# Half-height TensorE products made 128 rows high in a two-layer hybrid block

## The chip, the cores and the metric

The kernel runs on one core of a Trainium2 chip. The metric is the device time of one execution in microseconds (us); the time stated for a kernel is the median of its runs.

## The reference

Two layers over 512 latent tokens and 256 context tokens of width 1024. Each layer normalises its input, projects it with one matrix `w_in`, and feeds three token mixers: an RWKV-7 recurrence in both directions (4 heads of 64), a windowed attention with grouped queries (8 query heads on 2 key heads of 64, blocks of 128 tokens, a sink logit), and a 2-D Fourier mix. Their outputs are projected, weighted by sigmoid gates, summed and projected again; then comes a gated FFN with a convolution of width 3. The parts that the change touches:

```
for d, (xw, xa) in enumerate(((xw_f, xa_f), (xw_b, xa_b))):        # per direction
    w_log = -softplus(-(w0[d] + tanh(xw) @ w2[d])) - 0.5           # xw, xa: 64 columns each
    a = sigmoid(a0[d] + xa @ a2[d])
...
S = S * w_t + (S @ -kk_t) b_t^T + v_t k_t^T ;  y_t = S r_t         # recurrence, per head of 64
...
s_w = einsum("bqhgd,bkhd->bhgqk", q_b, k_b) * ATT_SCALE            # scores, d = 64
g = sigmoid(xg) @ g2                                               # gate of the recurrence's output
```

All is computed in float32; the large products run in a faster float32 form (named F32R in the code), each operand split in a high and a low part.

## The kernel before

All work is cut into 128-partition tiles; for each layer the order is: `w_in`'s first columns, the recurrence, the attention, the merge and output projection, the FFN. The code is straight-line Python without loops on the chip. Tiles come from pools with a fixed number of buffers, and a list scheduler sets the order of the instructions on each engine when the kernel is built, from the order of the program, the priorities (`tc.high_priority()` around the recurrence) and estimated durations. Once built, each engine works through its own list in order and waits on semaphores. DMAs are issued from SyncE (SP) in order, too.

**Background work.** The gates and branches of `mix` (`work`, a generator) and the modulation vectors (`bg`, `mods_few`) are interleaved with the recurrence and the attention. `wload` brings 128-column weights: a DMA to `wr`, ScalarE writes `wh`, GpSimd (POOL) or VectorE (DVE) writes `wl`; `gemm3` (L177 to L179) multiplies three times.

**The recurrence.** Tokens go in windows of 128, each direction d has one, six windows per layer (two of context, four of latents). `wkv_features` makes a window's operands: two LoRA products per direction (L808, over the 64 rows of direction d of `w2`, `a2`), activations, then for each head half h (rows 64h to 64h+63 hold one head of each pair) `W1[h]` (L846 on DVE, L848 on POOL) and `BK` (L849, L850 on DVE), four products `BK x W1[h]` over those 64 rows (L859), and DVE writes the masked results to `MR` (L864) and into the other 64 rows of `W1[h]` (L865), which `wkv_step` then uses at full height (L1016, L1042). `W1` has four buffers, so a window takes those of two windows before. `wkv_scan` inverts a small triangular matrix (`wkv_inverse`) and does two steps of 64 tokens (`wkv_prep`, `wkv_step`). Window w+1's features stand in the program ahead of window w's scan. `rwkv_readout` normalises the output and multiplies by a gate that comes from `g2` (L1098).

A float32 product stands in the trace as two weight loads and two matmuls; an F32R product as one of each.

**The scores.** `stacked` loads 64 rows of a query head twice, in partitions 0 to 63 and 64 to 127; the query tile holds the high part above and the low part below. The keys' `hi` is the high part in both halves, and `lo` the low part in the upper 64 rows alone. `scores` multiplies, for each of two heads and each group of key blocks, `qh` by `kh` over 128 rows (L1215) and by `kl` over the first 64 rows (L1216), adds masks (L1218) and the sink column (L1221). Softmax follows on DVE, ScalarE (ACT) and POOL, then `values` transposes (L1251) and multiplies (L1261) for the item before.

`cond` makes `sT` (SiLU of the conditioning vectors, 32 columns per k, of which two are not zero); TensorE reads it in `mods`, DVE as a scalar in `mods_bg` and `mods_few` (L293).

Of the kernel before, what the change touches and what calls it, by code (L numbers as in the profile page):

```python
# [7 lines left out]
F32 = mybir.dt.float32  # L8
# [3 lines left out]
ALU = mybir.AluOpType  # L12
# [8 lines left out]
KD = D // 128  # L21
# [42 lines left out]
class Kern:  # L64
# [117 lines left out]
    def setup(self):  # L182
# [18 lines left out]
        nc.gpsimd.memset(self.mT[1], 0.0)  # L201
        self.sT = self.t(cp, [128, KD, 32], "sT")
        self.mrow = [tc.dram_tile([3, 2, D], F32, name=f"mrow{l}") for l in range(DEPTH)]
# [4 lines left out]

    def cond(self):

        p = self.pool("condp", side="right")
        c = self.t(p, [128, 2, KD], "c")
        self.nc.sync.dma_start(out=c, in_=self.I["cond"])
        self.nc.vector.memset(self.sT, 0.0)
        self.act(self.sT[:, :, 0:2].rearrange("p k s -> p s k"), c, AF.Silu)
        p.release()

# [31 lines left out]
    def mods_bg(self, which, pool, tag="x", bufs=3):  # L249
# [3 lines left out]
        for l, r, ns in which:  # L253
            acc = [[self.t(pool, [128, 1024], "ma", bufs=4) for _ in range(2)] for _ in range(ns)]
            for k in range(KD):
                for g in range(2):
                    mw = self.t(pool, [128, 1024], "mw", bufs=bufs)
                    c0 = r * 2048 + g * 1024
                    nc.sync.dma_start(out=mw, in_=self.I["mod_w"][l, k * 128:(k + 1) * 128, c0:c0 + 1024])
                    for s in range(ns):  # L260
                        a, v = acc[s][g], self.sT[:, k, s:s + 1]
                        if k == 0:
                            nc.vector.tensor_scalar(a, mw, v, None, ALU.mult)
                        else:
                            nc.vector.scalar_tensor_tensor(a, mw, v, a, ALU.mult, ALU.add)
                    yield
# [9 lines left out]
    def mods_few(self, which, pool, tag):  # L276
# [3 lines left out]
        for l, r, c, ns in [(l, r, c, ns) for l, r, ns in which for c in range(8)]:  # L280
            c0 = r * 2048 + c * 256
            acc = [self.t(pool, [128, 256], "ma", bufs=4) for _ in range(ns)]
            for k in range(KD):
# [4 lines left out]
                for s in range(ns):  # L288
                    v = self.sT[:, k, s:s + 1]
                    if k == 0:  # L290
                        nc.vector.tensor_scalar(acc[s], mw[:, 0], v, None, ALU.mult)
                    else:
                        nc.vector.scalar_tensor_tensor(acc[s], mw[:, k % 4], v, acc[s], ALU.mult, ALU.add)  # L293
# [389 lines left out]
    def rwkv_params(self, l, pool):  # L683
        nc, I = self.nc, self.I
        w2 = self.t(pool, [128, RWKV_DIM], "w2")
        nc.sync.dma_start(out=w2, in_=I["rwkv_w2"][l].rearrange("d k c -> (d k) c"))
        a2 = self.t(pool, [128, RWKV_DIM], "a2")
        nc.sync.dma_start(out=a2, in_=I["rwkv_a2"][l].rearrange("d k c -> (d k) c"))
        g2 = self.t(pool, [128, RWKV_DIM], "g2")
        nc.sync.dma_start(out=g2, in_=I["rwkv_g2"][l])  # L690
        V = self.V1[l]
# [11 lines left out]
        if l > 0:  # L703
            nc.vector.tensor_scalar(x[:, 23:25], V[:, V_V0:V_V0 + 2], 0.5, None, ALU.mult)
        return dict(w2=w2, a2=a2, g2=g2, x=x)

# [70 lines left out]
    def wkv_features(self, l, w, F, P, wp, wt):  # L777
# [17 lines left out]
        for d in range(2):  # L795
# [5 lines left out]
            def tok(t):  # L801
                return flip(t[:, :, lo:lo + WT])

            pp = self.ps()
            for z, (lw, xx) in enumerate(((P["w2"], F["xw"]), (P["a2"], F["xa"]))):
                for k in range(2):
                    c = (2 * z + k) * WT
                    nc.tensor.matmul(pp[:, c:c + WT], lhsT=lw[64 * d:64 * d + 64, k * 128:(k + 1) * 128],  # L808
                                     rhs=xx[64 * d:64 * d + 64, lo:lo + WT], start=True, stop=True)
            sw = self.t(wt, [128, 2, WT], "wt")  # L810
# [22 lines left out]
            if need_y:  # L833
# [3 lines left out]
                else:  # L837
                    nc.gpsimd.tensor_tensor(kb, kb, kf, ALU.add)
            W1 = [self.t(wp, [128, NC, 2, 128], f"W1{h}", bufs=4) for h in range(2)]
            BK = self.t(wp, [128, NC, 2, 128], "BK", bufs=4)  # L840
# [15 lines left out]
            for h in range(2):  # L856
                ps = self.ps()
                for q in range(4):
                    nc.tensor.matmul(ps[:, q * 128:q * 128 + m], lhsT=rows(BK, h)[:, q // 2, q % 2, :],  # L859
                                     rhs=rows(W1[h], h)[:, q // 2, q % 2, 0:m], start=True, stop=True)  # L860
                pv = ps.rearrange("p (q t) -> p q t", q=4)[:, :, 0:m]
# [198 lines left out]
    def rwkv_readout(self, l, F, P, out, tmp):  # L1060
# [5 lines left out]
        parts = (("l", 0, TL), ("c", TL, TC))[:len(halves)]  # L1066
        n = TT if l == 0 else TL
        dv = self.t(tmp, [128, 2, TT], "dv", bufs=1)
        va = self.t(tmp, [128, 2, TT], "va", bufs=1)
# [15 lines left out]
        for k in range(2):  # L1085
# [10 lines left out]
            for o, w in halves:  # L1096
                ps = self.ps()
                nc.tensor.matmul(ps[:, :w], lhsT=P["g2"][:, k * 128:(k + 1) * 128], rhs=F["xg"][:, o:o + w], start=True,  # L1098
                                 stop=True)
# [56 lines left out]
    def stacked(self, src, o, n, pool, tag, bufs, keys=False):  # L1156
# [10 lines left out]
        lo = self.t(pool, [128, TT], tag + "l", F32R, bufs=bufs)  # L1167
        nc.vector.tensor_tensor(lo[0:64, :n], d[0:64, :n], hi[0:64, :n].bitcast(F32), ALU.subtract)
        return hi, lo
# [25 lines left out]
    def scores(self, l, t, i, qa, ka, pool):  # L1195
# [8 lines left out]
        for hh in range(2):  # L1204
# [4 lines left out]
            for first, n, c in ((blks[0], nw, c0), (4, 2, 512)):  # L1209
# [5 lines left out]
                nc.tensor.matmul(o, lhsT=qh[:, qs], rhs=kh[:, ks], start=True, stop=False)  # L1215
                nc.tensor.matmul(o, lhsT=qh[0:64, qs], rhs=kl[0:64, ks], start=False, stop=not masked)  # L1216
                for z in masked:
# [340 lines left out]
    def run(self):  # L1558
# [5 lines left out]
        p0 = self.pool("modp", side=B)  # L1564
        self.cond()
        tiles = []
# [234 lines left out]
```

## Time and profile before

| | |
|---|---|
| runs | 2569.32, 2578.45, 2600.42 us; median 2578.45 |
| the profiled execution | 2573.11 us, of which the span is 2571.3 us |
| mean granted TensorE clock | 0.948 of full |
| busy in the span | PE 93%, PEld 76%, DVE 73%, ACT 41%, POOL 37% |
| DMA | 251.35 MB, mean 98 GB/s |

PE is TensorE's matmuls and PEld its weight loads, which can run beside matmuls. A matmul's end is modelled and consecutive matmuls overlap in the profile, so the time that one takes out of a stream is read from the start of one to the start of the next (called its slot here), not from its duration. Times in the views are us from the span's start.

### The profile page before, as it was taken

The numbers are of one execution on the slowest core, as the hardware profiler recorded it, in microseconds if no ns is written. First come the engines' busy times: TensorE is split into PE (matmuls) and PEld (weight loads), VectorE is DVE, ScalarE is ACT, GpSimd is POOL, SyncE is SP. The second block draws the span as 40 slices with busy tenths as digits, with TensorE's granted clock in tenths as the row PEclk, the third lists the DMA queues.
The fourth block names the chain that finished last, engine by engine and source line by source line (L and its number), as shares of the span: only waits on it lengthen the run. The fifth ranks groups of instructions, "written<-read, shape, count | busy, mean of one in ns | idle before, by whom it ended". The sixth has DMA issues, their size and how long they took to land. (4 is left out here: it accounts for less than half of the span.)

```text
span 2571.3 us, 43544 instructions
## 1 busy us (share of the span) xinstructions
PE 2379.3 (93%) x16612; PEld 1957.7 (76%) x16612; DVE 1882.8 (73%) x3458; ACT 1054.6 (41%) x2156; POOL 941.1 (37%) x908
## 2 busy tenths in 40 slices
PE   7898999999999979999999888999989998899997
PEld 4766777787777768899898776667767776888886
DVE  5966776827765577878878845788666866999988
ACT  3243343334433445334333534435334434544443
POOL 4442322023333264333333543333123434545553
PEclk9988989999989989999999998789989999999999
DMA  7611111743324222122122421111264544333321
GB/s 236 191 50 44 48 41 36 221 129 116 117 80 144 95 70 79 58 69 72 60 74 64 135 86 58 54 46 59 63 207 142 155 129 138 105 96 99 99 87 58
DMA packets 284464, 251.35 MB, mean 98 GB/s; under 512 B 14460, under 2 KB 241236, under 8 KB 284256
## 3 DMA queue, kind: packets, MB, share of 16 engines
q1 hardware_dynamic: 284256, 248.57, 30.8%
q8 instruction: 131, 2.15, 0.3%
q14 instruction: 77, 0.63, 0.1%
HBM read 221.23 MB, written 27.29 MB: 97 GB/s over the span
## 5 line engine op out<-in xcount | busy, mean ns | idle before, releaser
L177 PE MATMUL mm<-at,wh 128*128 128x256 f32 (+2 forms) x1968 | 675.5, 344 | 15.8 <-DVE v L612 7.1
L179 PE MATMUL mm<-at,wl 128*128 128x256 f32 (+2 forms) x1968 | 670.7, 341 | 7.7 <-DVE wl L118 5.5
L178 PE MATMUL mm<-at,wh 128*128 128x256 f32 (+2 forms) x1968 | 668.9, 340 | 9.6 <-POOL at L118 6.9
L118 POOL TENSOR_TENSOR wl<-wr,wh 128x512 fp32r<-128x512 f32 (+1 forms) x248 | 343.1, 1390 | 490.8 <-ACT wh L106 459.2
L177 PEld LDWEIGHTS mm<-at,wh 128*128 128x128 f32 x1968 | 388.2, 197 | 53.4 <-issue 7.9
L178 PEld LDWEIGHTS mm<-at,wh 128*128 128x128 f32 x1968 | 387.5, 197 | 43.7 <-POOL at L118 10.8
L179 PEld LDWEIGHTS mm<-at,wl 128*128 128x128 f32 x1968 | 387.2, 197 | 36.8 <-DVE wl L118 7.3
L106 ACT ACTIVATE wh<-wr 128x512 fp32r<-128x512 f32 (+1 forms) x342 | 204.3, 605 | 229.3 <-PE mm L178 127.0
L118 DVE TENSOR_TENSOR wl<-ws,wh 128x512 fp32r<-128x512 f32 x176 | 166.8, 949 | 62.8 <-ACT wh L106 62.8
L177 PE MATMUL x<-dh,hid 128*128 128x512 f32 x440 | 177.7, 404 | 27.9 <-DVE acc L602 26.5
L293 DVE SCALAR_TENSOR_TENSOR ma<-mw,sT,ma 128x256 f32<-128x256 f32 x336 | 184.9, 590 | 11.7 <-DMA mw<-in_mod_w 9.1
L179 PE MATMUL x<-dh,hid 128*128 128x512 f32 x440 | 172.8, 394 | 1.1 <-DVE hid L118 1.1
L178 PE MATMUL x<-dl,hid 128*128 128x512 f32 x440 | 172.9, 393 | 0.0
L602 DVE TENSOR_TENSOR acc<-x,acc 128x512 f32<-128x512 f32 x200 | 134.4, 683 | 23.4 <-PE x L179 22.9
L118 POOL TENSOR_TENSOR dl<-dr,dh 128x1024 fp32r<-128x1024 f32 x44 | 112.0, 2545 | 81.6 <-ACT dh L106 76.6
L106 ACT ACTIVATE wh<-ws 128x512 fp32r<-128x512 f32 x170 | 103.7, 623 | 85.6 <-PE mm L178 67.5
L177 PEld LDWEIGHTS x<-dh,hid 128*128 128x128 f32 x440 | 83.1, 189 | 54.5 <-DVE acc L602 37.4
L106 ACT ACTIVATE P<-P,st 128x513 f32<-128x513 f32 (+5 forms) x120 | 86.1, 722 | 81.8 <-DVE P L1227 70.9
L178 PE MATMUL x<-at,wh 128*128 128x512 f32 (+2 forms) x312 | 114.9, 368 | 5.0 <-POOL at L118 3.0
L177 PE MATMUL x<-at,wh 128*128 128x512 f32 (+2 forms) x312 | 116.2, 373 | 1.5 <-DVE mT L311 0.8
L154 POOL TENSOR_TENSOR ws<-wr,wr 128x512 f32<-128x512 f32 x42 | 66.2, 1577 | 139.6 <-DVE wl L118 138.9
L179 PE MATMUL x<-at,wl 128*128 128x512 f32 (+2 forms) x312 | 114.8, 368 | 0.0
(486 smaller groups left out, 4811.9 us busy)
## 6 DMA issues: line engine op xcount, KB each, us to landing
mw<-in_mod_w SPq DMA_DIRECT2D x96, 512.0 KB
wr<-in_ffn_up SPq DMA_DIRECT2D x176, 256.0 KB
wr<-in_w_in SPq DMA_DIRECT2D x164, 256.0 KB
dr<-in_ffn_down SPq DMA_DIRECT2D x44, 512.0 KB
gd<-sg SPq DMA_DIRECT2D x32, 256.0 KB
wraw<-in_w_out SPq DMA_DIRECT2D x32, 256.0 KB
hd<-h SPq DMA_DIRECT2D x32, 256.0 KB
h<-hd SPq DMA_DIRECT2D x28, 256.0 KB
```

Of the source, the lines that this page charges most:

```text
L106: return self.nc.scalar.activation(out, in_, func, **kw)
L118: e.tensor_tensor(lo, full, hi.bitcast(F32), ALU.subtract)
L154: e.tensor_tensor(raw[m], raw[x], raw[y], op)
L177: mm(ps, lhsT=lh, rhs=rh, start=first and k == 0, stop=False)
L178: mm(ps, lhsT=lh, rhs=rl, start=False, stop=False)
L179: mm(ps, lhsT=ll, rhs=rh, start=False, stop=last and k == nk - 1)
L293: nc.vector.scalar_tensor_tensor(acc[s], mw[:, k % 4], v, acc[s], ALU.mult, ALU.add)
L602: nc.vector.tensor_tensor(acc[i][:, cs], ps, acc[i][:, cs], ALU.add)
```

## The change

`scores` multiplies `qh` by `kl` over all 128 rows, and `stacked` fills the lower 64 rows of `lo` as well. `w2` and `a2` get one copy per direction, each with 64 rows of zeros, so that L808 runs over 128 rows; the products of `BK` and `W1[h]` (L859) run over 128 rows, with `W1[h]`'s other 64 rows set to zero by POOL at the start of a direction's features. The load of `g2` moves from `rwkv_params` into `rwkv_readout`. `sT` moves into a pool that is released early, and `s2` keeps its two columns that DVE reads.

```diff
-        self.sT = self.t(cp, [128, KD, 32], "sT")
+        self.s2 = self.t(cp, [128, KD, 2], "s2")
...
-    def cond(self):
+    def cond(self, pool):
+        self.sT = self.t(pool, [128, KD, 32], "sT", bufs=1)
...
         self.act(self.sT[:, :, 0:2].rearrange("p k s -> p s k"), c, AF.Silu)
+        self.nc.gpsimd.tensor_copy(self.s2, self.sT[:, :, 0:2])
...
-        w2 = self.t(pool, [128, RWKV_DIM], "w2")
-        nc.sync.dma_start(out=w2, in_=I["rwkv_w2"][l].rearrange("d k c -> (d k) c"))
-        a2 = self.t(pool, [128, RWKV_DIM], "a2")
-        nc.sync.dma_start(out=a2, in_=I["rwkv_a2"][l].rearrange("d k c -> (d k) c"))
-        g2 = self.t(pool, [128, RWKV_DIM], "g2")
-        nc.sync.dma_start(out=g2, in_=I["rwkv_g2"][l])
+        w2, a2 = (self.t(pool, [128, 2, RWKV_DIM], m) for m in ("w2", "a2"))
+        for m, src in ((w2, I["rwkv_w2"]), (a2, I["rwkv_a2"])):
+            for d in range(2):
+                nc.gpsimd.memset(m[64 - 64 * d:128 - 64 * d, d], 0.0)
+                nc.sync.dma_start(out=m[64 * d:64 * d + 64, d], in_=src[l, d])
...
+            W1 = [self.t(wp, [128, NC, 2, 128], f"W1{h}", bufs=4) for h in range(2)]
+            for h in range(2):
+                nc.gpsimd.memset(rows(W1[h], 1 - h)[:, :, :, 0:m], 0.0)
...
-                    nc.tensor.matmul(pp[:, c:c + WT], lhsT=lw[64 * d:64 * d + 64, k * 128:(k + 1) * 128],
-                                     rhs=xx[64 * d:64 * d + 64, lo:lo + WT], start=True, stop=True)
+                    nc.tensor.matmul(pp[:, c:c + WT], lhsT=lw[:, d, k * 128:(k + 1) * 128], rhs=xx[:, lo:lo + WT],
+                                     start=True, stop=True)
...
-                    nc.tensor.matmul(ps[:, q * 128:q * 128 + m], lhsT=rows(BK, h)[:, q // 2, q % 2, :],
-                                     rhs=rows(W1[h], h)[:, q // 2, q % 2, 0:m], start=True, stop=True)
+                    nc.tensor.matmul(ps[:, q * 128:q * 128 + m], lhsT=BK[:, q // 2, q % 2, :],
+                                     rhs=W1[h][:, q // 2, q % 2, 0:m], start=True, stop=True)
...
+        g2 = self.t(tmp, [128, RWKV_DIM], "g2", bufs=1)
+        nc.sync.dma_start(out=g2, in_=self.I["rwkv_g2"][l])
...
-        nc.vector.tensor_tensor(lo[0:64, :n], d[0:64, :n], hi[0:64, :n].bitcast(F32), ALU.subtract)
+        nc.vector.tensor_tensor(lo[:, :n], d[:, :n], hi[:, :n].bitcast(F32), ALU.subtract)
...
-                nc.tensor.matmul(o, lhsT=qh[0:64, qs], rhs=kl[0:64, ks], start=False, stop=not masked)
+                nc.tensor.matmul(o, lhsT=qh[:, qs], rhs=kl[:, ks], start=False, stop=not masked)
```

## Rows read from the trace of the kernel before

**Rows 1.** The page's first part: busy time, share of the span, instructions.
```profile
PE 2379.3 (93%) x16612; PEld 1957.7 (76%) x16612; DVE 1882.8 (73%) x3458; ACT 1054.6 (41%) x2156; POOL 941.1 (37%) x908
```

**Rows 2.** Windows: length, busy (instructions) PE, PEld, DVE, ACT, POOL; clock; DMA.
```profile
565.00:805.00 240.00, 234.67 (x1485) 178.85 (x1484) 155.77 (x391) 102.42 (x233) 77.37 (x67) 0.97 0.35 107
1880.00:2085.00 205.00, 199.80 (x1140) 148.94 (x1140) 140.25 (x308) 88.73 (x185) 74.79 (x66) 0.97 0.51 156
140.00:480.00 340.00, 311.97 (x3504) 245.10 (x3503) 245.66 (x579) 137.85 (x324) 98.84 (x161) 0.89 0.19 59
1560.00:1880.00 320.00, 294.51 (x3130) 218.03 (x3130) 234.73 (x557) 139.06 (x321) 87.67 (x147) 0.87 0.21 66
```

**Rows 3.** Timeline of PE, one head's scores: start, us, then the instruction (rows*columns, operand).
```profile
638.62 0.28 PE L179 MATMUL x<-yh,wl 128*128 128x256 f32 x1
638.73 0.34 PE L1215 MATMUL s<-ka,qa 128*128 128x384 f32 x1
639.00 0.44 PE L1216 MATMUL s<-kal,qa 64*128 64x384 f32 x1
639.38 0.23 PE L1218 MATMUL s<-mprev,identb 128*128 128x128 bf16 x1
...
639.47 0.36 PE L1215 MATMUL s<-ka,qa 128*128 128x256 f32 x1
639.76 0.38 PE L1216 MATMUL s<-kal,qa 64*128 64x256 f32 x1
640.08 0.18 PE L1221 MATMUL s<-sink,onesb 128*128 128x1 bf16 x1
```

**Rows 4.** Timeline of PEld, the weight load of one second product.
```profile
639.00 0.18 PEld L1216 LDWEIGHTS s<-kal,qa 64*128 64x128 f32 x1 [0.19 <-issue]
```

**Rows 5.** Timeline of PE in the FFN, full-height products with 384 columns.
```profile
1004.73 0.34 PE L177 MATMUL mm<-at,wh 128*128 128x384 f32 x1
1004.90 0.34 PE L178 MATMUL mm<-at,wh 128*128 128x384 f32 x1
```

**Rows 6.** Groups by line and form: count, busy us, mean ns, idle before and its releasers.
```profile
L1216 PE MATMUL s<-kal,qa 64*128 64x256 f32 x112 | 44.0, 393 | 0.3 <-DVE kal L1168 0.3
L1216 PE MATMUL s<-kal,qa 64*128 64x384 f32 x32 | 15.1, 471 | 0.0
```

**Rows 7.** Timeline of PE in the recurrence: one group of eight, one of sixteen half-height matmuls.
```profile
303.70 0.71 PE L808 MATMUL x<-xw,w 64*128 64x128 f32 x4
304.25 0.61 PE L808 MATMUL x<-xa,a 64*128 64x128 f32 x4
304.79 0.50 PE L177 MATMUL mm<-at,wh 128*128 128x512 f32 x1
...
318.36 0.28 PE L178 MATMUL mm<-at,wh 128*128 128x256 f32 x1
318.57 1.71 PE L859 MATMUL x<-W,BK 64*128 64x128 f32 x16
320.21 0.39 PE L179 MATMUL mm<-at,wl 128*128 128x256 f32 x1
320.44 0.28 PE L177 MATMUL mm<-at,wh 128*128 128x256 f32 x1
```

**Rows 8.** Groups by line and form, L859 on PE: idle before it and releasers.
```profile
L859 PE MATMUL x<-W,BK 64*128 64x128 f32 x320 | 46.5, 302 | 22.8 <-DVE BK L850 13.5 <-POOL W L848 8.7 <-DVE BK L849 0.6
L859 PE MATMUL x<-W,BK 64*128 64x64 f32 x64 | 11.3, 332 | 9.3 <-DVE BK L849 5.8 <-DVE BK L850 3.4
```

**Rows 9.** Timeline of POOL: a memset, and the two products of one direction's features.
```profile
293.06 0.31 POOL L905 MEMSET T<- 128x256 f32 x1 [2.79 <-ACT iv L106]
...
299.44 1.71 POOL L848 TENSOR_TENSOR W<-r,e 64x256 f32<-64x256 f32 x2
```

**Rows 10.** Timelines of SP and PE at the start of layer 2's readout.
```profile
1860.35 1.40 SPq L1478 DMA_DIRECT2D back<-zd  x3
...
1868.94 0.70 PE L1098 MATMUL x<-xg,g 128*128 128x512 f32 x1 [0.35 <-DVE bo L1093]
```

More of the change, by code (lines that the diff above doesn't have):

```diff
@@ L260, in mods_bg @@
                     for s in range(ns):
-                        a, v = acc[s][g], self.sT[:, k, s:s + 1]
+                        a, v = acc[s][g], self.s2[:, k, s:s + 1]
                         if k == 0:
@@ L288, in mods_few @@
                 for s in range(ns):
-                    v = self.sT[:, k, s:s + 1]
+                    v = self.s2[:, k, s:s + 1]
                     if k == 0:
@@ L704, in rwkv_params @@
             nc.vector.tensor_scalar(x[:, 23:25], V[:, V_V0:V_V0 + 2], 0.5, None, ALU.mult)
-        return dict(w2=w2, a2=a2, g2=g2, x=x)
+        return dict(w2=w2, a2=a2, x=x)
     def shift(self, l, c, pl, pc, dst, x):
@@ L838, in wkv_features @@
                     nc.gpsimd.tensor_tensor(kb, kb, kf, ALU.add)
-            W1 = [self.t(wp, [128, NC, 2, 128], f"W1{h}", bufs=4) for h in range(2)]
             BK = self.t(wp, [128, NC, 2, 128], "BK", bufs=4)
@@ L1097, in rwkv_readout @@
                 ps = self.ps()
-                nc.tensor.matmul(ps[:, :w], lhsT=P["g2"][:, k * 128:(k + 1) * 128], rhs=F["xg"][:, o:o + w], start=True,
+                nc.tensor.matmul(ps[:, :w], lhsT=g2[:, k * 128:(k + 1) * 128], rhs=F["xg"][:, o:o + w], start=True,
                                  stop=True)
@@ L1564, in run @@
         p0 = self.pool("modp", side=B)
-        self.cond()
+        self.cond(p0)
         tiles = []
```

## The prediction

> **What bounds the kernel now.** The page comes first: PE is busy for 93% of the span, the next engine for 73% [rows 1]. That is an average, so the windows of the four stretches that the change touches come next. In the two attention stretches (565 to 805 and 1880 to 2085 us) PE is idle for 240 - 234.7 = 5.3 us and 205 - 199.8 = 5.2 us; DVE, the next, is busy for 65% and 68% [rows 2]. What PE no longer has to do there should come off the span. In the two recurrence stretches (140 to 480, 1560 to 1880) PE idles for 28.0 and 25.5 us, and the granted clock is 0.89 and 0.87 [rows 2]: a chain of waits takes part there. The groups by line tell where: 22.8 + 9.3 = 32.1 of those 53.5 us stand just before L859 and were ended by DVE's BK or POOL's W [rows 8].
>
> A busy PE isn't a well used one, so the third view is PE's timeline, read from start to start. A full-height product of 256 columns takes 0.11 us out of the stream (638.62 to 638.73) [rows 3], one of 384 columns 0.17 us [rows 5]. In the scores the pair of 384 columns takes 0.27 + 0.38 us, the pair of 256 columns 0.29 + 0.32 us [rows 3]. PEld's timeline says why: the second product's weight load starts at 639.00, together with its matmul, after 0.19 us in which PEld did nothing [rows 4]. On the way from 128 to 64 rows and on the way back the stream is emptied, and the next weight load isn't hidden.
>
> **Scores (certain in size, on the path).** There are 112 + 32 = 144 second products [rows 6], 80 in layer 1, 64 in layer 2. At full height the 384 pair should take 2 x 0.17 = 0.34 instead of 0.65: 0.31 less. In the 256 pair the first product follows a short bf16 product, whose own cover for the next weight load is small; I take its switch alone off it, which the 384 pair shows as 0.27 - 0.17 = 0.10, so 0.19 + 0.11 = 0.30 instead of 0.61: 0.31 less; to be careful 0.29 for all, since a few pairs are met at other neighbours. That is 144 x 0.29 = 41.8 us; 8 of the 144 lie beside a product of 64 columns, where one switch stays, so 41 us. It lies on PE in stretches where PE is idle for 2%: after it DVE would be busy for 156 of 217 us (72%) and 140 of 186 us (75%), so no other engine becomes the bound on average, but DVE and ACT hand each item's softmax back to PE, and in-order waits will grow a little. I count 90%: **-37 us** (bounds -41 and -14, the second if a third is left). DVE's subtraction in `stacked` covers 128 partitions instead of 64 in the same number of elements each: nothing, in the four that there are.
>
> **LoRA and BK products.** An isolated group of eight half-height matmuls takes 304.79 - 303.70 = 1.09 us instead of 8 x 0.11 = 0.88 (the slot of a 256-column product, so no less than what 128 columns need): 0.21 too much. The product ahead of such a group takes 318.57 - 318.36 = 0.21 instead of 0.11, and the one behind it 320.44 - 320.21 = 0.23 instead of 0.11 [rows 7]. Together 0.43. Along the timeline 36 groups stand so between full-height products (16 of L808, 20 of L859), which makes 15 us. Eight groups have L859's two halves in direct succession, as the sixteen at 318.57: from 318.36 to 320.44 they cost 2.08 us, less two ordinary products of 0.11 makes 1.86, against 16 x 0.11 = 1.76 at full height: 0.1 each, 1 us. The others lie beside products of 32 or 64 rows or columns, where a switch stays: 0. Of these 16 us PE can use only what isn't followed by a longer wait at L859, which hangs on ACT, DVE and POOL: half, **-8 us** (-16 to 0).
>
> Here a rule speaks against the change. In the sixteen, the fifth and later matmuls of one half and the first ones of the other do overlap: 1.64 us for sixteen against 1.09 for eight, so about 0.5 of 2.18 us was saved by it [rows 7]. The Trainium skill (TensorEngine Tiling, section Row Tiling under When to Use Tiling, and the overview's Theoretical Speedup) says that products with at most 64 rows should be put on separate row tiles, up to twice as fast. By that rule the 24 sixteens would cost up to 24 x 0.88 = 21 us more at full height; by the rows, 0.1 us less in the eight that do meet. The halves mostly don't meet in this order of work, and the rows decide.
>
> **Zeros in W1, on POOL.** 6 windows x 2 directions x 2 halves x 2 layers = 48 memsets, 40 of 512 and 8 of 256 elements per partition. A memset of 256 elements takes 0.31 us [rows 9]; 512 I put at 0.55 (between 0.31 and twice 0.31): 24.5 us of POOL time. POOL has room (99 of 340 us, 88 of 320 us busy) [rows 2], but it works in order: a memset must wait until the scan of two windows before has read W1 for the last time (L1042), and L848 of the same direction, which PE waits for, waits for the same buffer. So the memsets of a direction (1.1 us) can land just ahead of L848 (1.71 us for its two) [rows 9]; queued behind them are also `Zp` (L1011) and background `wl`. PE's idle time ended by L848 is 8.7 of 32.1 us [rows 8], so POOL is last in about a quarter of cases: 24 x 1.1 x 0.25 = 7 us, less what the built order moves out of the way: **+4 us** (0 to +26).
>
> **L859 waits for both halves of BK.** It reads all 128 rows, so the first half's products wait for the second half's L850. If both were waiting anyway, what is added is the first half's own products, 0.88 us, at most 24 times: +21 us. DVE's BK ended 13.5 + 0.6 + 9.3 = 23.4 us of waits at L859 [rows 8], so such waits are common, but the order of PE is built with the new dependence, and background products can stand before it: **+4 us** (0 to +21). L865 now overwrites rows that L859 read; it needs all of that product's result already, so nothing.
>
> **Clock.** At 0.89 and 0.87 the recurrence stretches lose 0.11 x 340 + 0.13 x 320 = 79 us of full-speed time [rows 2], in half-speed stretches of some microseconds, about half of which begin behind L859 or L808 groups with a wait. Whether full height counts for the clock no row shows, since the rows added are zeros. If waits grow, it loses more; if groups shorten, less: **-2 us** (-25 to +10).
>
> **The rest.** `w2` and `a2` become four loads of half the size per layer instead of two, among loads that stand 80 us ahead of their use; four memsets of 256 elements per layer, 1.2 us of POOL in a loading phase; `s2`, one small copy: 0. `g2` is now loaded in the readout. Its space is that of the recurrence's pools, so SP holds it, and what is queued behind it, until the last step is done, as it does today for `back` at 1860.35; L1098 needs it at 1868.94, 8.6 us later [rows 10]. Three loads of 1.40 us issue time fit in between: 0 (0 to +3).
>
> **The sum.** -37 - 8 + 4 + 4 - 2 = -39. The profiled execution took 2573.1 us (span 2571.3, 1.8 around it), 5.3 below the median of the three runs, which spread over 31 us. 2573 - 39 = 2534; runs after will spread upward as well, so I put the median at 2537.
>
> **Rivals.** (1) *Attention is paced by softmax, not by PE.* Once PE is faster, P reaches the transposes later than PE does, and PE waits. For it: DVE and ACT form a chain through every item. Against: PE idles only 10.5 us in 445, and DVE is at 65 to 68% [rows 2]. If a third of the 41 us comes through: 2573 - 14 - 2 = 2557.
> (2) *The recurrence pays more than the scores give.* The mechanism is POOL's place in the chain: memsets wait for the last read of W1, L848 comes after them, L859 waits for both halves, and DVE, the inverse and the next scan follow. Each of 12 windows has 4 memsets (2.2 us) and 2 x 0.88 us of first-half products: up to 47 us if all is on the path, while its PE gain is void. Together with rival 1's 14 us from the scores this gives 2573 + 47 - 14 = 2606, slower than before. It decides from 3 us per window onwards (37 / 12).
> (3) *Full rows keep the clock up.* If the half-speed stretches behind L859 and L808 go, about half of 79 us comes back, of which 30 us reach the end: 2534 - 30 = 2504. For it: those stretches begin right there. Against: the waits themselves remain. The Trainium skill (TensorE: Matmul & The Clock Gate, Part 1) says that the clock follows how busy the array has lately been, and names no rows; no run here shows it yet.
> (4) *The switch doesn't come from the rows.* Then nothing is saved, the memsets remain: 2575. Against: L1215 and L1216 differ only in rows, and take 0.27 and 0.38 where full-height products take 0.17 [rows 3, 5].
>
> **Chances.** Forecast 0.60, rival 1 0.18, rival 2 0.06, rival 3 0.13, rival 4 0.03. The forecast's own range, from the bounds, is 2518 to 2556. For 8 in 10 the range takes in rival 1 and part of rival 3: 2508 to 2564. 2% of 2578 is 52 us, about what a measurement here can tell from no change: below 2527 is faster. A quarter of the forecast's cases and all of rival 3 lie there, and a little of the shuffled order of background work: 0.32. Slower than 2630 needs rival 2 at more than its price: 0.02. Same: 0.66.
>
> **What would show it.** In the trace after, L1216 should have 128 rows, a slot of 0.11 (256 columns) or 0.17 (384), and its weight load should start ahead of its matmul; the two attention stretches should be some 20 and 17 us shorter with PE still above 95% busy. L808 and L859 should have slots near 0.11 throughout. Idle time before L859 should stand near 32 us, up to 40; if it is above 60, rival 2 is at work; if attention's PE share falls below 92%, rival 1. The clock in the recurrence should stay at 0.87 to 0.90. The prediction would be wrong, too, if the new instructions made the scheduler order background work otherwise, which no row can tell.

## The result and the profile after

The changed kernel took 2512.97 us (median of 4 runs, 2510.79 to 2514.14), the kernel before in the same comparison 2582.98 (4 runs, 2569.32 to 2600.42). The ratio is 0.972 with an interval of 0.966 to 0.979: faster by 2.8%. The forecast was 2537, with a range of 2508 to 2564. So sign and range held, and the likeliest value was 24 us too high; a change this clear (below 2527 us) had been given a chance of 0.32, no clear change 0.66. The profiled execution took 2513.85 us (span 2511.9) against 2573.11: 59 us less where 39 were forecast, at a mean granted clock of 0.965 against 0.948.

The page's first part of the kernel after answers to [rows 1]:

```profile
PE 2293.3 (91%) x16612; PEld 1923.1 (77%) x16612; DVE 1889.0 (75%) x3458; ACT 1052.8 (42%) x2153; POOL 965.1 (38%) x965
```

PE has 86 us less to do with as many instructions, and the span fell by 59: some of what PE gave back became waiting. Windows show where. The first two lines are the attention stretches of the kernel before, cut at the first score and the last product of values (columns as in [rows 2]):

```profile
583.00:803.00 220.00, 214.73 (x1363) 161.33 (x1363) 149.22 (x380) 94.20 (x216) 71.62 (x61) 0.97 0.34 105
1917.00:2081.00 164.00, 162.71 (x973) 118.14 (x971) 114.67 (x262) 75.18 (x161) 64.63 (x56) 0.96 0.48 149
```

the same stretches of the kernel after:

```profile
572.00:770.00 198.00, 189.10 (x1368) 153.05 (x1368) 150.68 (x380) 94.14 (x217) 71.88 (x61) 1.00 0.39 117
1872.00:2018.00 146.00, 141.61 (x964) 111.55 (x963) 111.64 (x260) 75.27 (x161) 64.10 (x55) 0.98 0.56 167
```

The recurrences, from the first LoRA product to the last product with `MR`, before:

```profile
149.00:451.00 302.00, 275.73 (x3337) 218.19 (x3336) 216.66 (x516) 118.56 (x296) 90.60 (x144) 0.88 0.14 43
1568.00:1859.00 291.00, 269.98 (x3051) 203.51 (x3051) 215.94 (x522) 123.10 (x299) 84.97 (x142) 0.86 0.18 54
```

and after:

```profile
148.00:443.00 295.00, 260.68 (x3336) 212.56 (x3336) 218.04 (x516) 118.30 (x297) 99.38 (x173) 0.92 0.16 49
1539.00:1817.00 278.00, 248.21 (x3066) 193.08 (x3065) 219.29 (x521) 124.84 (x301) 97.30 (x163) 0.93 0.19 59
```

Each length can be split in three: idle time (length less PE's busy time), time lost to the clock (length times 1 - clock), and the rest, the work as it would be at full speed.

| | length | idle | lost to the clock | rest |
|---|---|---|---|---|
| attention before | 384 | 6.6 | 13.2 | 364 |
| attention after | 344 | 13.3 | 2.9 | 328 |
| recurrence before | 593 | 47.3 | 77.0 | 469 |
| recurrence after | 573 | 64.1 | 43.1 | 466 |

Attention: 40 us shorter, of which 36 are work and 10 the clock, less 7 of new waits. Recurrence: 20 us shorter, of which 34 are the clock and 3 work, less 17 of new waits. All else together changed by about 1 us: the two FFN stretches are some 4 us longer each, the stretches between are shorter. (The clock is read to two digits, so each of its terms may be off by 1 or 2 us. Where PE was idle while the clock stood at half, this split counts the time twice: by the records of the granted clock that is 7.5 us of the recurrence before and 12.0 after, so the recurrence's work hardly shrank at all and the clock's part is some 36.)

What the switch was forecast to cost can be read off. PE's timeline in the scores of the kernel after, beside [rows 3]:

```profile
609.42 0.23 PE L1225 MATMUL s<-mnext,identb 128*128 128x128 bf16 x1
609.46 0.36 PE L1222 MATMUL s<-ka,qa 128*128 128x256 f32 x1
609.66 0.28 PE L1223 MATMUL s<-kal,qa 128*128 128x256 f32 x1
609.78 0.18 PE L1228 MATMUL s<-sink,onesb 128*128 128x1 bf16 x1
```

The pair of 256 columns, behind a short bf16 product as in [rows 3], takes 0.20 + 0.12 us instead of 0.29 + 0.32. PEld's timeline answers to [rows 4]:

```profile
609.42 0.20 PEld L1222 LDWEIGHTS s<-ka,qa 128*128 128x128 f32 x1
609.54 0.19 PEld L1223 LDWEIGHTS s<-kal,qa 128*128 128x128 f32 x1
```

L1223's load starts at 609.54, 0.12 us ahead of its matmul at 609.66. Over all pairs of the two traces at full clock the medians are 0.61 and 0.32 us for 256 columns, 0.73 and 0.44 for 384: 0.28 to 0.29 less for each, where the prediction put 0.29. In the recurrence, PE's timeline beside [rows 7]:

```profile
309.85 0.28 PE L178 MATMUL mm<-at,wh 128*128 128x256 f32 x1
309.97 1.95 PE L864 MATMUL x<-W,BK 128*128 128x128 f32 x16
311.67 0.36 PE L179 MATMUL mm<-at,wl 128*128 128x256 f32 x1
311.87 0.28 PE L177 MATMUL mm<-at,wh 128*128 128x256 f32 x1
...
344.24 0.61 PE L814 MATMUL x<-xw,w 128*128 128x128 f32 x4
344.68 0.61 PE L814 MATMUL x<-xa,a 128*128 128x128 f32 x4
345.05 0.47 PE L177 MATMUL mm<-at,wh 128*128 128x512 f32 x1
```

The eight take 0.81 us (1.09 before). The sixteen with their neighbours take 311.87 - 309.85 = 2.02 us (2.08 before): where both halves already met, almost nothing was to be had. Last, the groups of BK's products by form, beside [rows 8]:

```profile
L864 PE MATMUL x<-W,BK 128*128 128x128 f32 x320 | 50.8, 323 | 35.4 <-DVE BK L855 23.0 <-POOL W L853 8.7 <-DVE BK L854 3.6
L864 PE MATMUL x<-W,BK 128*128 128x64 f32 x64 | 11.3, 351 | 12.1 <-DVE BK L854 6.3 <-DVE BK L855 5.8
```

PE now waits 47.5 us there instead of 32.1. All of the growth is DVE's BK; POOL's W ends 8.7 us of waits, as it did before.

### The profile page after: what moved, and what is told of

It reads as the page before. It is cut to its first block, busy times and chain, and to the rows that moved or that the text cites. A ratio compares the mean times of both kernels' runs of the same rounds, so it can differ in the third digit from the quotient of the medians.

```text
span 2511.9 us, 43604 instructions
## 1 busy us (share of the span) xinstructions
PE 2293.3 (91%) x16612; PEld 1923.1 (77%) x16612; DVE 1889.0 (75%) x3458; ACT 1052.8 (42%) x2153; POOL 965.1 (38%) x965
## 5 line engine op out<-in xcount | busy, mean ns | idle before, releaser
L177 PE MATMUL mm<-at,wh 128*128 128x256 f32 (+2 forms) x1968 | 661.8, 337 | 14.4 <-DVE v L614 7.0
L178 PE MATMUL mm<-at,wh 128*128 128x256 f32 (+2 forms) x1968 | 660.5, 336 | 12.8 <-POOL at L118 7.3
L179 PE MATMUL mm<-at,wl 128*128 128x256 f32 (+2 forms) x1968 | 659.7, 336 | 8.2 <-DVE wl L118 5.9
L177 PEld LDWEIGHTS mm<-at,wh 128*128 128x128 f32 x1968 | 380.8, 194 | 46.9 <-issue 5.6
L178 PEld LDWEIGHTS mm<-at,wh 128*128 128x128 f32 x1968 | 381.1, 194 | 43.4 <-POOL at L118 10.0
L179 PEld LDWEIGHTS mm<-at,wl 128*128 128x128 f32 x1968 | 380.9, 194 | 34.4 <-DVE wl L118 8.9
L295 DVE SCALAR_TENSOR_TENSOR ma<-mw,s,ma 128x256 f32<-128x256 f32 x336 | 187.3, 597 | 11.0 <-DMA mw<-in_mod_w 8.2
L154 POOL TENSOR_TENSOR ws<-ws,wr 128x512 f32<-128x512 f32 x42 | 62.8, 1495 | 132.5 <-DVE wl L118 75.0
```

What stands on the lines that cost most here:

```text
L154: e.tensor_tensor(raw[m], raw[x], raw[y], op)
L177: mm(ps, lhsT=lh, rhs=rh, start=first and k == 0, stop=False)
L178: mm(ps, lhsT=lh, rhs=rl, start=False, stop=False)
L179: mm(ps, lhsT=ll, rhs=rh, start=False, stop=last and k == nk - 1)
```

## The experiments

The theory after the result: two things happened. The switch between 64 and 128 rows went out of the scores, and the recurrence's products at 128 rows kept TensorE's clock up, zeros or not (the third rival's mechanism). The main rival: the recurrence gained nothing of its own, and what the clock shows is chance or the order into which the scheduler happened to put the background products.

**Scores alone.** The kernel before with the two lines of the scores:

```diff
-        nc.vector.tensor_tensor(lo[0:64, :n], d[0:64, :n], hi[0:64, :n].bitcast(F32), ALU.subtract)
+        nc.vector.tensor_tensor(lo[:, :n], d[:, :n], hi[:, :n].bitcast(F32), ALU.subtract)
...
-                nc.tensor.matmul(o, lhsT=qh[0:64, qs], rhs=kl[0:64, ks], start=False, stop=not masked)
+                nc.tensor.matmul(o, lhsT=qh[:, qs], rhs=kl[:, ks], start=False, stop=not masked)
```

> Before with the scores' change alone (second product and the keys' low part at 128 rows). The theory that the gain is the array's switch between 64 and 128 rows expects the two attention stretches to shorten by about 41 us together, as in the changed kernel, and the rest to stay: 2583 - 41 = 2542 us. The rival that a good part of those 41 us is the clock, whose half-speed stretches in the attention went away by luck of the order, expects 20 to 30 us: 2553 to 2563.

Measured: 2543.01 us against 2576.78, ratio 0.986 (0.981 to 0.991): 34 us, between the 41 of the switch alone and the 20 to 30 of the rival. In the trace PE's products stand in the same order as before, so no new order is mixed into it. The attention windows:

```profile
600.00:799.00 199.00, 190.32 (x1368) 154.24 (x1369) 150.46 (x380) 94.37 (x217) 71.20 (x61) 0.99 0.38 117
1902.00:2050.00 148.00, 144.62 (x975) 114.42 (x974) 115.05 (x262) 75.24 (x162) 64.76 (x56) 0.97 0.55 166
```

347 us against 384; 6.4 are lost to the clock (13.2 before) and 12.1 are idle (6.6 before). So the switch itself brings 37 - 7 = 30 us net of the clock. The recurrence, whose code is that of before, stood in this execution at 0.83 and 0.91 instead of 0.88 and 0.86:

```profile
146.00:467.00 321.00, 293.09 (x3324) 231.07 (x3322) 219.12 (x518) 119.25 (x297) 90.67 (x147) 0.83 0.13 41
1565.00:1845.00 280.00, 256.64 (x3054) 193.89 (x3053) 217.10 (x521) 122.43 (x298) 85.07 (x140) 0.91 0.18 56
```

One stage's clock in one execution can thus be off by 0.05, and what the clock did has to rest on medians of several runs.

**Everything but the scores.** The kernel after with those two lines as before:

> The changed kernel with the scores' second product back at 64 rows: only the recurrence's part, with zeros, loads and moved tiles. The switch theory, as forecast, expects nothing much from it (0 to -10 us: 2573 to 2583), since half of the 16 us of PE time would go into waits and zeros would cost some. The rival that full rows keep the clock up expects -20 to -35 us: 2548 to 2563, with a granted clock in the recurrence stretches of 0.92 or more against 0.89 and 0.87.

Measured: 2551.95 us, ratio 0.989 (0.985 to 0.992): 25 us, in runs whose clocks were 0.959 to 0.962, as the clock's rival expected. In the trace PE's order is that of the kernel after, so the scores' lines on top of it bring 2552 - 2513 = 39 us. Alone the two parts give 34 + 25 = 59 us, together 2577 - 2513 = 64; the 5 us between are not explained.

**The scaffold.** The same, and the products of L814 and L864 at 64 rows again; the zeros, the four loads, `g2`'s and `sT`'s new places are kept:

```diff
...
-                    nc.tensor.matmul(ps[:, q * 128:q * 128 + m], lhsT=BK[:, q // 2, q % 2, :],
-                                     rhs=W1[h][:, q // 2, q % 2, 0:m], start=True, stop=True)
+                    nc.tensor.matmul(ps[:, q * 128:q * 128 + m], lhsT=rows(BK, h)[:, q // 2, q % 2, :],
+                                     rhs=rows(W1[h], h)[:, q // 2, q % 2, 0:m], start=True, stop=True)
...
```

> The changed kernel with all products back at 64 rows: what is left is the zeros in W1 and in the LoRA weights, the four loads, the late gate load and the two-column copy. Nothing of it saves PE time. The theory that zeros on POOL cost expects +4 to +26 us: 2587 to 2609. The rival that the new order of instructions alone makes part of the gain expects a time below before, 2560 to 2575.

Measured: 2590.23 us, ratio 1.006 (1.003 to 1.008), clocks 0.937 to 0.945. That lies in the range of the case in which zeros cost (2587 to 2609); the runs on the zeros below take it up. Against the scaffold, full height is worth 2590 - 2552 = 38 us; but the order of PE's products differs between the two, and against the scaffold without zeros (2573.78 us, below) it is 22. The recurrence windows, first of the scaffold:

```profile
147.00:459.00 312.00, 283.76 (x3336) 226.34 (x3337) 216.49 (x518) 118.04 (x298) 98.93 (x174) 0.85 0.13 42
1582.00:1873.00 291.00, 267.96 (x3054) 201.69 (x3055) 215.37 (x522) 122.89 (x299) 94.67 (x161) 0.87 0.17 54
```

then with full height:

```profile
148.00:440.00 292.00, 258.33 (x3350) 210.89 (x3349) 217.94 (x517) 118.26 (x297) 99.31 (x173) 0.93 0.16 50
1558.00:1835.00 277.00, 243.66 (x3051) 189.31 (x3051) 219.57 (x520) 124.48 (x300) 96.74 (x161) 0.95 0.19 59
```

603 us became 569. The time lost to the clock went from 46.8 + 37.8 = 84.6 to 20.4 + 13.9 = 34.3, 50 us less, while idle time rose from 51.3 to 67.0. The stretch waits more and is yet shorter: the gain isn't fewer stalls.

The records of the granted clock in these windows tell where it fell. In the profiles before and after it fell 18 and 13 times; the falls that came within 5 us behind products of BK or LoRA were 13 and 5, and held half speed for 102 and 24 us, all others for 51 and 61. So there the whole gain lies behind the products that were made full height. Between scaffold and full height it lies there in part: 75 and 34 us behind such products, 96 and 34 elsewhere.

**Streams without waits.** A kernel that computes nothing of the reference: streams of matmuls with nothing to wait for, each after a warming stretch.

> A small kernel of its own, which computes nothing of the reference: streams of products without a wait, each behind a stretch of full products of 512 columns. First float32 products of 128 columns with 64 rows, then the same with 128 rows, then with 128 rows of which 64 are zero in both operands, then F32R products of 512 columns with 32 rows, then with 128 rows of which 96 are zero. If the granted clock asks how many rows are addressed, the first and the fourth stream fall to 0.5 and the second, third and fifth hold 1.0. If it asks only whether the array is streaming, the first three behave alike, and the last two hold 1.0. If zero operands count as no work, the third and fifth behave as the first and fourth.

Windows, in the order 64 rows, 128 rows, 128 rows of which 64 are zeros (128 columns each), then 32 rows and 128 rows of which 96 are zeros (512 columns, F32R):

```profile
28.00:72.00 44.00, 44.00 (x395) 44.00 (x396) 0.00 (x0) 0.00 (x0) 0.00 (x0) 1.00 0.00 1
93.00:137.00 44.00, 44.00 (x394) 43.95 (x393) 0.00 (x0) 0.00 (x0) 0.00 (x0) 1.00 0.00 1
158.00:202.00 44.00, 44.00 (x395) 43.92 (x394) 0.00 (x0) 0.00 (x0) 0.00 (x0) 1.00 0.00 1
224.00:283.00 59.00, 59.00 (x148) 44.98 (x148) 0.00 (x0) 0.00 (x0) 0.00 (x0) 0.54 0.00 0
307.00:340.00 33.00, 33.00 (x147) 27.31 (x146) 0.00 (x0) 0.00 (x0) 0.00 (x0) 1.00 0.00 0
```

A stream of 64-row products is as fast as one of 128 rows (395 and 394 matmuls in 44 us): half height costs nothing, the change of height does. It also held 1.00, so rows alone don't decide: by the first of the three cases above it should have fallen. But the stream of 32 rows fell to the lower level (1.2 GHz) without a single wait in it, while the same data in 128 rows, 96 of them zeros, stayed at 2.4 GHz.

**Bursts with waits.** The recurrence has waits between its products, so: nine products of 512 columns, a wait for DVE, 24 times over, with four ways to fill the rows. It computes nothing of the reference either.

> A small kernel of its own, which computes nothing of the reference: bursts of nine F32R products of 512 columns, each followed by a wait for two DVE instructions, 24 times in each of four sections: with 64 rows; with 128 rows of which 64 are zero in both operands; with 128 full rows; and with twice nine products of 64 rows, upper and lower half of the array in turn. If the granted clock asks for the rows addressed, the first section falls to 0.5 and the second and third hold 1.0, though waits and columns are the same; the fourth holds 1.0 if two halves at once count as a full array. If it asks only how long the array is streaming, all four behave alike.

Windows: 64 rows; 128 rows with 64 zeros; 128 full rows; both halves of 64 rows in turn, 18 products a burst:

```profile
22.00:147.00 125.00, 96.35 (x216) 64.28 (x215) 25.68 (x46) 0.00 (x0) 0.00 (x0) 0.52 0.00 0
163.00:248.00 85.00, 56.33 (x218) 38.73 (x216) 25.70 (x46) 0.00 (x0) 0.00 (x0) 1.00 0.00 0
262.00:347.00 85.00, 56.39 (x219) 38.89 (x217) 25.71 (x46) 0.00 (x0) 0.00 (x0) 1.00 0.00 0
361.00:446.00 85.00, 56.29 (x435) 38.91 (x433) 25.71 (x46) 0.00 (x0) 0.00 (x0) 1.00 0.00 1
```

In these bursts, with the same columns and the same waits, the clock follows the rows that are addressed, and zeros count like data. At 64 rows it fell and stood at half (0.52 over the window), with zero rows it held 1.00. More idle time isn't what lowered it: PE was idle for 29 us in the first section, 29 in the second (at half clock the same products take longer, hence the 77% against 66% busy). The Trainium skill (TensorE: Matmul & The Clock Gate, Part 1) says that the clock follows how busy PE has been recently; here two sections of as many products and waits differ in rows alone, so the measurement goes further than the page. The last line holds the clock as well, and does twice the products in the same 85 us (435 against 219). The Trainium skill (TensorEngine Tiling (Array Packing), Theoretical Speedup) gives up to twice the speed for a dimension of at most 64; the trace agrees for these bursts, in which no full-height product stands. Each section ran once.

**BK at 64 rows, without zeros.** The kernel after, with the scaffold's two lines and no memset of W1:

> The changed kernel with the BK x W1 products back at 64 rows and without the zeros in W1; scores and LoRA products stay at 128 rows. If the recurrence's gain is the array's switches, 20 of its 36 groups return at 0.43 us, of which half shows, and the zeros' price (up to 15 us) falls away: 2505 to 2518 us. If it is the granted clock, most comes back here, since the half-speed stretches begin behind these products: clock 0.955 to 0.958 and 2525 to 2540 us.

Measured: 2544.85 us, ratio 0.989 (0.985 to 0.994), clocks 0.944 to 0.949. This is 5 us above the clock's case and far from the other. BK's products with their zeros are worth 2545 - 2513 = 32 us, the difference in order included.

**LoRA at 64 rows.** The kernel after, L814 as in the scaffold; in the trace PE's order is that of the kernel after:

```diff
-                    nc.tensor.matmul(pp[:, c:c + WT], lhsT=lw[:, d, k * 128:(k + 1) * 128], rhs=xx[:, lo:lo + WT],
-                                     start=True, stop=True)
+                    nc.tensor.matmul(pp[:, c:c + WT], lhsT=lw[64 * d:64 * d + 64, d, k * 128:(k + 1) * 128],
+                                     rhs=xx[64 * d:64 * d + 64, lo:lo + WT], start=True, stop=True)
```

> The changed kernel with the LoRA products alone back at 64 rows. Switches: 16 groups of 0.43 us return, half of it shows: 2515 to 2520 us. Clock: few half-speed stretches begin behind these products, so 2515 to 2525 us with a clock of 0.960 to 0.964.

Measured: 2512.82 us, ratio 0.976 (0.972 to 0.980), clocks 0.962 to 0.965. Both cases had expected it slower; the LoRA part is worth nothing, though PE's timeline shows its eight shorter by 0.28 us.

**Halves in turn.** BK's products at 64 rows and without zeros, but the two halves written alternately into two PSUM tiles:

```diff
...
+            pss = [self.ps() for _ in range(2)]
+            for q in range(4):
+                for h in range(2):
+                    nc.tensor.matmul(pss[h][:, q * 128:q * 128 + m], lhsT=rows(BK, h)[:, q // 2, q % 2, :],
...
```

> As the kernel with BK products at 64 rows and no zeros, but with the two halves' products issued in turn, so that an upper and a lower half of the array can work at once. The rule that half-height products belong on separate row halves expects sixteen matmuls in some 0.9 to 1.1 us instead of 1.76 and a time at or below the changed kernel, 2500 to 2513 us. If the clock decides, the time is near that of the plain half-height version or between the two, 2515 to 2535 us, as the array is full for half as long.

Measured: 2535.76 us, ratio 0.985 (0.981 to 0.990), clocks 0.951 to 0.957. But the scheduler mostly put the halves one after the other again, so the run is no test of halves at once. Products of the two halves that run at once start together (0.003 us apart in the last section of the bursts). Here, of 16 groups of sixteen, 11 have no two products that start together; only the one at 328.09 has most of them in pairs:

```profile
328.09 1.49 PE L861 MATMUL x<-W,BK 64*128 64x128 f32 x16
329.50 0.38 PE L179 MATMUL mm<-at,wl 128*128 128x256 f32 x1
...
1754.88 2.26 PE L861 MATMUL x<-W,BK 64*128 64x128 f32 x16 [1.57 <-DVE BK L852]
1757.07 0.50 PE L177 MATMUL mm<-at,wh 128*128 128x512 f32 x1
```

That group takes 1.41 us, the other one 2.19; none is near 0.9 to 1.1. The 9 us to the halves one after the other are no more than an order alone can move (below), and whether halves truly in turn would match full height stays open.

**Useless full-height products.** The kernel after, with four products of no use ahead of each of BK's halves, to fill the waits there:

```diff
                 ps = self.ps()
+                for _ in range(4):
+                    nc.tensor.matmul(ps[:, 0:128], lhsT=self.onesbd, rhs=W1[h][:, 0, :, 0:64], start=True, stop=True)
                 for q in range(4):
```

> The changed kernel with four more full-height float32 products of 128 columns ahead of each group of four BK x W1 products, whose result is overwritten: 192 products, 384 matmuls of 0.11 us, 42 us more work for TensorE and none of use. They need W1 alone, so they run in the wait for BK. If the recurrence is bound by TensorE's work and switches, it gets slower by 10 to 42 us: 2523 to 2555. If the granted clock decides, the dips behind these waits go, the clock rises to 0.970 or more, and the time is the same or lower in spite of the work: 2495 to 2515 us.

Measured: 2557.10 us, ratio 0.993 (0.991 to 0.996), clocks 0.964 to 0.967. I had expected 2495 to 2515; this missed by over 40 us. Groups by line:

```profile
L864 PE MATMUL x<-W,table 128*128 128x128 f32 x384 | 60.8, 300 | 38.0 <-DVE W L851 31.7 <-POOL W L809 6.3
L866 PE MATMUL x<-W,BK 128*128 128x128 f32 x320 | 46.4, 293 | 3.3 <-DVE BK L855 2.1 <-POOL W L853 1.0 <-DVE BK L854 0.2
```

The fill read W1 and so waited itself: 38 us moved one instruction forward, and all of its work was added. The clock barely rose (0.9645 to 0.966). By the ranges set ahead this is the rival's side, 2 us past its end. But the products ran behind the waits and not in them, so the run counts neither for the clock nor against it.

**The zeros: none, on DVE, and twice.** Three kernels: the scaffold without the memsets of W1, the kernel after with them on DVE, and the kernel after with each done twice.

> All products at 64 rows, and the scaffold of the change without the zeros in W1 (48 memsets less than in the scaffold run, 21 us of POOL). If the zeros are what the scaffold costs (15 us there), this stands within 5 us of before: 2570 to 2580 us. If the cost lies in the moved tiles, loads and order, it stays at 2585 to 2592 us.

> The changed kernel with the zeros in W1 written by DVE instead of POOL. If POOL's place in the chain costs the zeros' price, this is faster by up to 10 us: 2503 to 2513 us. If DVE's own waits at the BK products grow by the same, it is the same or slower: 2513 to 2525 us.

> The changed kernel with every zeroing of W1's other rows done twice on POOL: 48 more memsets of 0.52 us, 24 us more of POOL's time, at the place where the product of W on POOL is next. Theory (what the zeros cost in the scaffold, about 15 us, they cost in the changed kernel too, since POOL is late there just as often): a second set costs about as much again, 2513 + 15 = 2528 us. Rival (in the changed kernel the longer waits for BK cover the zeros): 2513 to 2517 us. Idle time of PE before the BK products ended by POOL's W would grow from 8.7 us to some 15 to 25 us by the theory, and stay by the rival.

Measured: the scaffold without zeros 2573.78 us (12 runs), ratio 1.000 (0.997 to 1.003), 16 less than with them; zeros on DVE 2517.07, ratio 0.979 (0.976 to 0.983); zeros twice **2501.54**, ratio 0.970 (0.967 to 0.974). Had I stopped at the first, I would have said that the zeros cost 16 us. But POOL's W ended 9.9 us of waits in the scaffold with them and 8.8 without, and the mean clocks (0.941 and 0.9495) are by themselves worth 17 us at the price given below. The zeros on DVE came out as the second case had it. With a second set the kernel took 2493 to 2510 us, less than each run of the kernel after (2511 to 2514): 11 us faster in the medians, so both theory and rival of that last run missed the time. Its groups, beside those of the kernel after, show the waits unchanged (47.1 us against 47.5), 10.6 of them by POOL's W (8.7 there), which is nearer to the rival:

```profile
L865 PE MATMUL x<-W,BK 128*128 128x128 f32 x320 | 50.3, 322 | 38.3 <-DVE BK L856 23.7 <-POOL W L854 10.6 <-DVE BK L855 4.0
L865 PE MATMUL x<-W,BK 128*128 128x64 f32 x64 | 8.0, 279 | 8.8 <-DVE BK L856 7.9 <-DVE BK L855 0.9
```

What else differs is the order: with other instructions on POOL the scheduler places background products elsewhere (812 of PE's 16,612 products fall out of the common order in the traces, 907 between the scaffolds with and without zeros). This is the fastest version measured, but the second set of zeros computes nothing in it; how far its gain is the order and how far the clock (0.967) stays open.

**Is it the order, then?** Orders differ between most of these kernels, so the rival has to be met by counting. With BK at 64 rows there were four different orders. Their clocks, as means of the timed runs: 0.949 (the kernel before; scores alone has its order and 0.9505), 0.941 (scaffold), 0.9495 (scaffold without zeros; BK at 64 rows has its order and 0.946) and 0.9545 (halves in turn). With BK at 128 rows there were four too: 0.9645 (the kernel after; without the scores 0.9605, LoRA at 64 rows 0.964), 0.961 (zeros on DVE), 0.966 (useless products) and 0.967 (zeros twice). The two sets don't overlap; were the rows without effect, chance would sort four against four so once in 70 times. The gap between them (0.9545 to 0.9605) is smaller than what order does within the first (0.941 to 0.9545), and no run changes BK's rows and keeps the order. So the rival is unlikely, but not shut out, and the sizes below hold to within what an order moves.

What a clock is worth comes from the kernel before itself: over its 52 fast runs beside these experiments, from 0.941 to 0.958, the time falls by 2.0 us per 0.001 (correlation -0.92). From the scaffold to full height 0.9412 to 0.9605 gives 39 us (measured 38), from BK at 64 to 128 rows 0.946 to 0.9645 gives 37 (measured 32).

## Why the prediction was right in sign and range, and 24 us too high

**Scores, -37:** 40 in the profiled attention stretches, 34 and 39 in the two clean pairs. The switch's own part, net of the clock, is 30 (scores alone) to 36 - 7 = 29 (the profile after): the work shrank by 36 where the prediction put 41 on PE, and waits took 7 where it allowed 4. The clock, of which this step said nothing, gave 7 to 10 back; why, no run separates. The slots were nearly as forecast (0.32 us for a pair put at 0.30), PE's share stayed at 189.1 / 198 = 96% and 97%, and rival 1 is out.

**LoRA and BK switches, -8, and waiting for both halves, +4:** The rows were right for the slots (0.81 for an eight, 2.02 for a sixteen with neighbours), yet at full speed the recurrence's work shrank by 3 us at most where 16 were counted on PE, and the waits before L864 grew by 15 where 4 were allowed. "Half is lost to waits" was too mild: all of it and more was. Idle time before these products (47.5 us) went past the 40 that the prediction had allowed. DVE's BK ended all of the growth, POOL's W none. How much is the wait for both halves, and how much PE merely arriving sooner at a chain that DVE sets, the runs don't separate. Returning LoRA to 64 rows changed nothing. One reading was wrong, too: the 0.5 us that sixteen products save against twice eight isn't mainly the halves' overlap. In the stream of 64-row products a matmul takes 44 / 395 = 0.111 us, so sixteen take 1.78 without any overlap, against 1.64; the rest is that the height changes once instead of twice.

**Zeros, +4:** 23.3 us of POOL time in 48 memsets were forecast as 24.5, and the waits for POOL's W stayed at 8.7. So rival 2's path over POOL did not appear; the term is 0 as far as POOL's waits go.

**Clock, -2: this step failed.** It measured 34 us in the recurrence and 7 to 10 in the attention. The prediction asked whether zero rows count, found no row of the trace that shows it, and took a value near nothing, although 13 of the 18 falls of the clock in the recurrence came within 5 us behind the groups of 64 rows. Zero rows do count in the bursts: with 64 rows alone they fell to half, with zero rows beside them they held 1.00. The prediction's own sign failed: the recurrence's clock was to stay at 0.87 to 0.90 and rose to 0.92 and 0.93. That was rival 3, given 0.13. Its mechanism fits what the runs show, and so does the size of what the clock gives back (30 us were put down for it); the end isn't 2504, because the switch term of the recurrence turned into waits.

**The rest, 0:** the moved loads and copies were hidden, as the scaffold without zeros shows (2573.78 against 2576.35 for the kernel before). The FFN's 8 us more remain unexplained: 5 of them are idle time of PE, and the scores alone, with the order of before, don't have them.

So the range held, near its lower end, by two errors of opposite sign, which is luck in part: 22 us too hopeful on switches and waits (8 in the scores, 14 in the recurrence), some 41 too careful on the clock.

## What to carry to other kernels

Where products of 64 rows stand among full-height ones, padding them with rows of zeros can be worth more than their PE time says: it takes out the change of height, and it can keep the clock up, so look at the granted clock behind such groups before putting that term at nothing. Read a gain as work, idle time and clock separately, since here one of them paid for another. And before naming an added instruction as a cost, add it twice: the kernel moved by 11 to 16 us with the order that the scheduler built around such additions, once up and once down.

## What the runs showed of the hardware beyond that

A stream of 32-row products at 512 columns fell to half speed without any wait in it (0.54 over 59 us, PE busy throughout); a stream of 64-row products of 128 columns did not. A stream of 64-row products costs the same per product as one of 128 rows (395 and 394 in 44 us); the change between heights costs time (0.61 us for a pair of scores against 0.32), as the next weight load then starts with its matmul instead of ahead of it. One stage's clock in one execution of unchanged code differed by 0.05 (0.83 and 0.88).
